# A four-layer trunk on one core: pooling bands made on GpSimd, a new order of the first loads and mixer steps, and last sums kept in PSUM

## Chip, core and metric

The kernel runs on one core of one Trainium2 chip. The metric is the device time of one execution in microseconds; less is better. Besides it the text uses one profiled execution, whose instructions are recorded with start, duration and what released them. Engines are named as in the profile: PE is TensorE, PEld its weight loads, DVE is VectorE, ACT is ScalarE, POOL is GpSimd, SP is SyncE, from which nearly all transfers are issued.

## The reference, cut to what matters

512 tokens of width 1024 go through two layers. The first mixes tokens by causal averages, the second by stick-breaking attention; a squared-ReLU MLP with 4096 hidden units follows each. All is float32, and RMS norms stand before and after each part:

```python
x = x + rms_norm(m, mix_post_g[layer])
h = rms_norm(x, mlp_pre_g[layer])
x = x + rms_norm(sq_relu_mlp(h, w_up[layer], w_down[layer]), mlp_post_g[layer])
```

The mixer of the first layer averages each of four groups of 256 channels over the last 2, 4, 8 or 16 tokens (fewer at the start of the sequence), subtracts the token itself, and applies a 256x256 linear map and a scale per channel:

```python
count = jnp.minimum(pos + 1, w).astype(jnp.float32)[None, :, None]
outs.append((upper - lower) / count - hf[:, :, sl])
...
y = jnp.einsum('bsgc,gcd->bsgd', y, w_grp.astype(jnp.float32)).reshape(B, S, D)
```

## The kernel before, in words

Tokens are cut into four tiles of 128 (`xt[0]` to `xt[3]`, kept on chip throughout). Float32 products of the MLPs and of the attention are made of three fast products of a high and a low part, so each operand is split by a ScalarE cast (high) and a VectorE subtraction (low).

**The mixer (lines 736 to 890).** An average over a window is a matrix product with a band: `own[t]` holds, for the four windows, 128 columns of weights for the tokens of the same tile and 16 columns for what reaches into the next tile (`BW` = 144, 576 columns in all). The bands come from the host as constants: one for tile 0, where the counts are smaller, and one for the later tiles, each 128 x 576 (lines 742, 750, 755). A tile's band is scaled by its inverse norm (line 809). `pooled` multiplies the tile with it (line 817), `copied` brings the result out of PSUM on ScalarE (line 827), `reached` adds the columns from the tile before (line 834), `mixed` applies the linear map (line 845), whose weights `pw` are first multiplied on VectorE by the gain and the scale (`linear`, line 788). The scale arrives as one row and is spread over the partitions by a product with ones (lines 777, 780). Norms run as ScalarE squares with an accumulator (line 301), two small GpSimd instructions (total, line 305, and power, line 312), and products on VectorE (349, 367, 403). Then tiles are transposed (411), split (421, 430) and meet the first up weights; `half_up` (line 870) starts four blocks of the first MLP on tiles 0 and 1.

The order of TensorE, ScalarE, VectorE and GpSimd in the mixer is written out in `MIX_ORDER` (line 45): each word is a step, a letter and indices. z: warm-up matmuls, so many; r, e: scale row and its copy; q, v, b: squares of x, inverse norm and scaled band of a tile; p, c, f, m: pooled, copied, reached and mixed of a tile and a part; w: linear weights of a half; s, g, V, a: squares, product with the gain, inverse norm and addition of the update; S, W, n: the same for the norm after it; t, h, l: transposes, high and low part; i, k: high and low part of an up weight, u: its product on half the tokens; X: like V, with its total on VectorE. Each engine takes its own steps in that order and waits at the head of its queue. Transfers are issued from SP in an order that the planner chose; the trace shows the two halves of x0, first band, scale row, x1, identity and gain columns (`eye`), first half of `pw`, second band, second half of `pw`, x2, x3, two gain rows, and then four up weights (lines 137 and 748 to 760, 857).

**The end (finish, line 466).** The second MLP's last partial sums are made in the order of `MLP_ORDER[1]` (line 99). p: products of a tile and a column group; v: their sum with the partial result `y` in SBUF, on VectorE, written to `y` (line 483); s: squares on ScalarE; g: product with the gain row on VectorE (line 349); V: inverse norm on GpSimd; a: addition to x on VectorE and the transfer of the result, issued from SP. Tile 3 has three column groups, of 512, 256 and 256, so that little is left after the last product; its sum of squares is made of the first two groups' total and the third's (line 361). VectorE's queue around the last tiles is v20, a10, a11, g20, v21, g21, v30, g30, v31, a20, v32, a21, g31, g32, a30, a31, a32.

Of the kernel before, what the change touches and what calls it, by code (L numbers as in the profile page):

```python
# [22 lines left out]
GRP = 4  # L23
# [6 lines left out]
WINDOWS = (2, 4, 8, 16)  # L30
EPS = 1e-6
TINY = 1e-24
TS = [slice(t * P, (t + 1) * P) for t in range(T)]
# [13 lines left out]
    for w in """z11 q00 r1 q01 v0 r0 q1 b0 v1 p00 b1 p01 p02 e0 e1 c01 c00 w0 w1 c02 p10 c10 q2 p12 q3 p11 m00 v2 s00 b2 c11 f10  # L47
    m01 v3 p21 p20 c12 s01 b3 c21 V0 p22 f11 c20 m10 g01 g00 m11 p32 c22 a00 i0 i2 a01 s10 f20 s11 k0 p31 S00 k2
    S01 p30 c30 g11 g10 V1 W0 a11 f21 a10 c32 n01 S11 m20 c31 n00 S10 f31 s20 m21 s21 W1 g20 g21 f30 V2 t01 n10
    t00 n11 h00 h01 m31 l01 a20 t10 s31 l00 h10 t11 m30 l10 h11 S20 i1 l11 g30 s30 a21 S21 V3 k1 W2 g31 a30 u0  # L50
    a31 i3 u1 n21 n20 S30 S31 W3 t21 n31 t20 u2 n30 t30 h20 k3 h21 t31 l21 h30 l20 l30 h31 l31 u3""".split()
# [38 lines left out]
def last_steps(text):  # L90
# [9 lines left out]
    p110123 v11 s11 g11 V1 p200123 v20 s20 a10 a11 g20 p210123 v21 s21 g21 V2 p300123 v30 s30 g30  # L100
    p310123 v31 s31 a20 p320123 v32 s32 V3 a21 g31 g32 a30 a31 a32"""),
# [9 lines left out]
def trunk(ctx, tc, x, consts, grow, pw, wup, wdn, wq, wk, wv, wo, out):  # L111
# [37 lines left out]
    def spare_tile():  # L149
        return work.tile([P, D], F32, tag="spare", name=name("spare"))  # L150

    def gain_row(r, t=None):
        t = work.tile([P, D], F32, tag="grow", name=name("grow")) if t is None else t
        nc.sync.dma_start(t, grow[r : r + 1, :].broadcast_to((P, D)))
        return t
# [172 lines left out]
    class Update:  # L328
        def __init__(self, t, gpost, scaled, eps=EPS, gpre=None, final=False, xn=None, gcol=None):

            self.t, self.gpost, self.scaled, self.eps = t, gpost, scaled, eps
            self.gpre, self.gcol, self.final = gpre, gcol, final
            self.xn = xn_tile() if xn is None else xn
            self.st = keep.tile([P, 8], F32, tag=f"stat{t}", bufs=4, name=name("stat"))
            self.summed = False
# [11 lines left out]
        def product(self, n, y):  # L347
            cut = self.cuts[n]
            return nc.vector.tensor_tensor(out=self.scaled[:, cut], in0=y, in1=self.gpost[:, cut], op=ALU.mult)
# [5 lines left out]
        def first_rstd(self):  # L355
            if len(self.cuts) == 2:
                if not self.summed:
                    self.first_total()
            else:
                both = self.st[:, 2:3]  # L360
                nc.gpsimd.tensor_tensor(out=both, in0=both, in1=self.st[:, 4:5], op=ALU.add)
            self.summed = False
            self.r = power(self.st, 0)

        def add_part(self, n):
            x, cut = xt[self.t], self.cuts[n]
            latest["dve"] = nc.vector.scalar_tensor_tensor(  # L367
                out=x[:, cut], in0=self.scaled[:, cut], scalar=self.r, in1=x[:, cut], op0=ALU.mult, op1=ALU.add
            )

# [95 lines left out]
    def finish(l, lhs, w, y, update):  # L466

        ups = [update(t, y[t]) for t in range(T)]
        bank = {}
# [11 lines left out]
        def evacuate(t, n):  # L481
            part = y[t][:, ups[t].cuts[n]]
            nc.vector.tensor_tensor(out=part, in0=bank.pop((t, n)), in1=part, op=ALU.add)  # L483

        def add(t, n):
            ups[t].add_part(n)
            if l == 1:
                cut = ups[t].cuts[n]
                nc.sync.dma_start(out[TS[t], cut], xt[t][:, cut])

        def transposes(t, h):
# [4 lines left out]
            "s": lambda t, n: ups[t].squares_of(n, y[t][:, ups[t].cuts[n]]),  # L496
            "g": lambda t, n: ups[t].product(n, y[t][:, ups[t].cuts[n]]),
# [238 lines left out]
    with tc.tile_pool(name="mix0", bufs=1, reuse_waits="tile") as mp:  # L736
        warm = mp.tile([P, 512], mybir.dt.bfloat16, tag="warm", name="warm")
        nc.gpsimd.memset(warm, 0.0)


        BW = P + max(WINDOWS)
        bands = [mp.tile([P, 4 * BW], F32, tag=f"band{i}", name=f"band{i}") for i in range(2)]

        row = mp.tile([P, D], F32, tag="row", name="row")
        nc.vector.memset(row, 0.0)
        ones = mp.tile([P, P], F32, tag="ones", name="ones")
        nc.gpsimd.memset(ones, 1.0)
        nc.sync.dma_start(row[:1], grow[R_SCALE : R_SCALE + 1, :])
        at = P + 4 * KC
        nc.sync.dma_start(bands[0], consts[:, at : at + 4 * BW])  # L750
        nc.sync.dma_start(xt[1], x[TS[1], :])
        nc.sync.dma_start(eye, consts[:, :at])
        wpool = [mp.tile([P, D], F32, tag=f"pw{i}", name=f"pw{i}") for i in range(2)]
        nc.sync.dma_start(wpool[0], pw[0])
        nc.sync.dma_start(bands[1], consts[:, at + 4 * BW :])
        nc.sync.dma_start(wpool[1], pw[1])
        nc.sync.dma_start(xt[2], x[TS[2], :])
        nc.sync.dma_start(xt[3], x[TS[3], :])
        gpost = gain_row(R_MIX_POST0)
        gpre0 = gain_row(R_MLP_PRE0, spare_tile())  # L760

# [44 lines left out]
        def band(t):  # L806

            own[t] = mp.tile([P, 4 * BW], F32, tag=f"own{t}", name=f"own{t}")
            nc.vector.tensor_scalar(
                out=own[t], in0=bands[min(t, 1)], scalar1=left.pop(("v", t)), scalar2=None, op0=ALU.mult  # L810
            )

        def pooled(t, i):
            left["p", t, i] = ps()
            for c, cb in enumerate(BLOCKS[i]):
                g = cb // 2
                nc.tensor.matmul(  # L817
                    left["p", t, i][:, c * BW : (c + 1) * BW], xt[t][:, cb * P : (cb + 1) * P],
                    own[t][:, g * BW : (g + 1) * BW], start=True, stop=True,
                )  # L820
# [47 lines left out]
        def half_up(j):  # L868
# [5 lines left out]
            "b": band, "p": pooled, "c": copied, "f": reached, "m": mixed,  # L874
# [10 lines left out]
        for j in range(GRP):  # L885
            load_up(j)
# [413 lines left out]
def constants(gains):  # L1300


    s, t = np.arange(P)[:, None], np.arange(P)[None, :]
    eye = (s == t).astype(np.float32)
    first, later = [], []
    for w in WINDOWS:
        inside = ((s <= t) & (s > t - w)).astype(np.float32)
        before = ((s - P > t - w).astype(np.float32) / np.float32(w))[:, : max(WINDOWS)]
        first.extend((inside / np.minimum(t + 1, w).astype(np.float32) - eye, before))
        later.extend((inside / np.float32(w) - eye, before))  # L1310
    return np.concatenate([eye, gains, *first, *later], axis=1).astype(np.float32)
# [43 lines left out]
```

## Time and profile before

| | us |
|---|---|
| median of three runs | 946.03 |
| lowest and highest | 945.78 and 946.63 |
| the profiled execution | 945.7 |
| its span, first to last instruction | 943.9 |

The page of the profile gives, for each engine, busy time, share of the span and number of instructions. Views of the trace list single instructions by time, group them by line, or tell what ended the idle time before them. In a row `L809` is a line of the kernel, `own<-band,stat` the tile written and the tiles read, `128x576 f32` partitions by elements. A matmul's recorded duration includes the time in which the next already runs.

### The profile page before, as it was taken

How to read it: one execution, taken by the hardware profiler on the slowest of the kernel's cores; microseconds unless marked ns; L12 is line 12 of the kernel's file. 1: busy time of each engine (PE TensorE's matmuls, PEld its weight loads, DVE VectorE, ACT ScalarE, POOL GpSimd, SP SyncE). 2: the span in 40 equal slices, each digit the busy share in tenths (PEclk: the TensorE clock that was granted, in tenths of full speed). 3: DMA queues.
4: the chain of work that ended last, by engine and by line, in shares of the span. 5: the costliest groups of instructions: out<-in, count | busy, mean ns of one | idle time of the engine just before them, and what ended most of it. 6: DMA issues, size and time to landing. Idle time of an engine off the chain costs nothing.

```text
span 943.9 us, 12327 instructions
## 1 busy us (share of the span) xinstructions
PE 934.5 (99%) x4691; PEld 788.0 (83%) x4691; DVE 696.4 (74%) x797; ACT 560.2 (59%) x983; POOL 40.5 (4%) x83
## 2 busy tenths in 40 slices
PE   9999999999999999999999999999999999999997
PEld 7998888888888888888889888898888888888886
DVE  5875799988979876268766388884696966958756
ACT  6568979788775547155545464875545444444532
POOL 2300000000000004000000001200000000000002
PEclk9999999999999999999999999999999999999999
DMA  8334969789697750633141271342414133133102
GB/s 311 138 138 154 342 218 356 287 280 356 216 329 283 281 195 2 223 134 134 72 178 64 107 273 45 141 150 97 172 45 148 76 133 112 45 134 112 39 7 90
DMA packets 43261, 156.14 MB, mean 165 GB/s; under 512 B 4289, under 2 KB 4673, under 8 KB 43202
## 3 DMA queue, kind: packets, MB, share of 16 engines
q1 hardware_dynamic: 43202, 155.36, 45.4%
q8 instruction: 37, 0.61, 0.3%
q14 instruction: 22, 0.18, 0.1%
HBM read 121.79 MB, written 33.55 MB: 165 GB/s over the span
## 4 chain that ended last, share of the span: by engine, by line
PE 97%; DMA 1%; DVE 0%; ACT 0%; POOL 0%; SPq 0%; issue 0%; POOLq 0%; DVEq 0%; ACTq 0%
PE ps L605 28%; PE ps L727 16%; PE ps L728 16%; PE ps L724 15%; PE ps L317 4%; PE ps L316 4%; PE ps L318 4%; PE ps L1064 2%; PE ps L1047 2%; PE ps L1089 2%; PE ps L845 1%; PE ps L411 1%; PE ps L817 1%; DMA band<-in_consts 1%; ACT xn L301 0%; DVE x L367 0%
## 5 line engine op out<-in xcount | busy, mean ns | idle before, releaser
L605 PE MATMUL ps<-w,a 128*128 128x512 f32 x1176 | 278.6, 389 | 0.0
L727 PE MATMUL ps<-xnh,w 128*128 128x512 f32 (+1 forms) x704 | 260.5, 372 | 0.0
L728 PE MATMUL ps<-xnl,w 128*128 128x512 f32 (+1 forms) x704 | 259.9, 370 | 0.0
L724 PE MATMUL ps<-xnh,w 128*128 128x512 f32 (+1 forms) x704 | 259.0, 370 | 0.0
L605 PEld LDWEIGHTS ps<-w,a 128*128 128x128 f32 x1176 | 220.7, 188 | 45.9 <-DVE w L298 0.2
L728 PEld LDWEIGHTS ps<-xnl,w 128*128 128x128 f32 x704 | 132.7, 188 | 22.3 <-DVE xnl L430 0.3
L724 PEld LDWEIGHTS ps<-xnh,w 128*128 128x128 f32 x704 | 132.1, 188 | 22.7
L727 PEld LDWEIGHTS ps<-xnh,w 128*128 128x128 f32 x704 | 132.2, 188 | 22.4
L614 DVE TENSOR_TENSOR y<-ps,y 128x512 f32<-128x512 f32 x124 | 84.3, 687 | 44.7 <-PE ps L605 44.4
L177 DVE TENSOR_TENSOR w<-raw,w 128x1024 fp32r<-128x1024 f32 x58 | 70.9, 1222 | 57.0 <-ACT w L175 56.8
L175 ACT CAST w<-raw 128x1024 fp32r<-128x1024 f32 x58 | 60.9, 1051 | 80.9 <-PE ps L724 79.5
L297 ACT CAST a<-r 128x768 fp32r<-128x768 f32 (+1 forms) x60 | 47.7, 794 | 71.8 <-PE ps L605 56.8
L298 DVE TENSOR_TENSOR a<-r,a 128x768 fp32r<-128x768 f32 (+1 forms) x60 | 54.0, 900 | 11.8 <-ACT a L297 11.6
L1028 DVE TENSOR_TENSOR_SCAN e<-u,begin 128x1280 f32<-128x1280 f32 x16 | 45.2, 2825 | 20.9 <-ACT u L1012 20.1
L297 ACT CAST w<-e 128x1536 fp32r<-128x1536 f32 (+1 forms) x30 | 41.8, 1395 | 22.7 <-DVE e L579 13.3
L298 DVE TENSOR_TENSOR w<-e,w 128x1536 fp32r<-128x1536 f32 (+1 forms) x30 | 49.4, 1647 | 1.8 <-ACT w L297 1.6
L187 ACT ACTIVATE apart<-apart,eye 128x128 f32<-128x128 f32 (+1 forms) x132 | 43.1, 408 | 0.0
L637 ACT ACTIVATE r<-ps 128x512 f32<-128x512 f32 x56 | 33.1, 591 | 8.7 <-PE ps L724 8.7
L298 DVE TENSOR_TENSOR w<-xn,w 128x1536 fp32r<-128x1536 f32 (+1 forms) x20 | 33.0, 1650 | 5.6 <-ACT w L297 5.5
L298 DVE TENSOR_TENSOR w<-w,w 128x1536 fp32r<-128x1536 f32 (+1 forms) x20 | 33.0, 1649 | 4.7 <-ACT w L297 4.7
L638 ACT ACTIVATE r<-r 128x512 f32<-128x512 f32 x56 | 35.5, 634 | 1.3
L301 ACT ACTIVATE xn<-y 128x512 f32<-128x512 f32 (+1 forms) x25 | 15.3, 614 | 31.6 <-DVE y L483 27.9
(134 smaller groups left out, 1321.4 us busy)
## 6 DMA issues: line engine op xcount, KB each, us to landing
raw<-in_wup SPq DMA_DIRECT2D x64, 512.0 KB, 4.1
w<-kept SPq DMA_DIRECT2D x60, 512.0 KB, 4.1
kept<-wx SPq DMA_DIRECT2D x30, 512.0 KB, 3.7
w<-in_wdn SPq DMA_DIRECT2D x8, 1536.0 KB, 6.6
kept<-apart SPq DMA_DIRECT2D x24, 512.0 KB, 5.7
xn<-in_wdn SPq DMA_DIRECT2D x8, 1536.0 KB, 7.4
apart<-in_wk SPq DMA_DIRECT2D x7, 512.0 KB, 7.2
apart<-in_wq SPq DMA_DIRECT2D x7, 512.0 KB, 9.5
```

The source lines that it names most:

```text
L175: nc.scalar.copy(hi, raw)
L177: nc.vector.tensor_tensor(out=lo, in0=raw, in1=hi.bitcast(F32), op=ALU.subtract)
L187: nc.scalar.mul(c, c, gc[:, at : at + 1])
L297: latest["act"] = nc.scalar.copy(hi, src)
L298: latest["dve"] = nc.vector.tensor_tensor(out=lo, in0=src, in1=hi.bitcast(F32), op=ALU.subtract)
L316: nc.tensor.matmul(dst, ah, bh, start=start, stop=False)
L605: nc.tensor.matmul(bank, a[:, x, q, TS[t]], w[:, z, q], start=start and q == 0 and k == 0, stop=q == self.n - 1 and k == 2, skip_group_che ...
L614: nc.vector.tensor_tensor(out=part, in0=bank, in1=part, op=ALU.add)
L724: nc.tensor.matmul(pu[:, cols], wl[:, k, :], xnh[:, k, cols], start=False, stop=k == KC - 1)
L727: nc.tensor.matmul(pu[:, cols], wh[:, k, :], xnh[:, k, cols], start=k == 0, stop=False)
L728: nc.tensor.matmul(pu[:, cols], wh[:, k, :], xnl[:, k, cols], start=False, stop=False)
L1028: nc.vector.tensor_tensor_scan(out=self.e[:, ::-1], data0=self.u[:, 1:][:, ::-1], data1=begin[:, ::-1], initial=0.0, op0=ALU.mult, op1=ALU ...
```

## The change

It has two parts that do not touch each other.

At the start, the bands are no longer sent from the host. VectorE fills `band` with the reciprocals of the windows, GpSimd cuts it to the band by one select over all four windows (below the diagonal) and one for each (beyond the window), makes a diagonal by another select, and VectorE subtracts it. What differs for the first 16 tokens is made in `first`, filled by 26 one-column memsets, and written over the first columns of tile 0's scaled band by a second instruction. The ones are filled by VectorE. The first loads are issued in a fixed order, and the four up weights only behind the last gain row. `MIX_ORDER` is listed anew, with eight warm-up matmuls in place of eleven and X0 in place of V0.

At the end, the sums of tiles 2 and 3 are written back into PSUM (`within`), where squares, gain product and addition read them. The sum of tile 3's two totals moves from GpSimd to VectorE. Tile 3's last column group is added to x by ScalarE (product with the inverse norm) and GpSimd (`add_apart`, step A); its second group's result is issued from ScalarE's queue. `MLP_ORDER[1]` places a20, a21 and g30 otherwise.

```diff
-    for w in """z11 q00 r1 q01 v0 r0 q1 b0 v1 p00 b1 p01 p02 e0 e1 c01 c00 w0 w1 c02 p10 c10 q2 p12 q3 p11 m00 v2 s00 b2 c11 f10
...
+    for w in """z8 q00 q01 v0 r0 q1 b0 r1 e0 v1 e1 p00 p01 b1 c00 c01 p02 q2 v2 p12 p11 w0 p10 c02 c11 w1 m00 m01 q3 c10 c12 b2
+    s01 s00 p21 v3 b3 g00 c21 p22 g01 f11 X0 p20 i0 m11 f10 a01 m10 a00 c20 p32 c22 i2 s11 g11 f20 k0 s10 S00
+    p31 S01 f21 V1 m21 p30 g10 W0 k2 a11 a10 m20 c31 c32 n01 S11 n00 f31 t00 c30 S10 s21 t01 s20 m31 g21 g20 h01
...
-    p110123 v11 s11 g11 V1 p200123 v20 s20 a10 a11 g20 p210123 v21 s21 g21 V2 p300123 v30 s30 g30
-    p310123 v31 s31 a20 p320123 v32 s32 V3 a21 g31 g32 a30 a31 a32"""),
+    p110123 v11 s11 g11 V1 p200123 v20 s20 a10 a11 g20 p210123 v21 s21 V2 g21 a20 p300123 v30 s30 a21 p310123
+    v31 s31 g30 p320123 v32 s32 g31 V3 g32 a30 A32 a31"""),
...
-                nc.gpsimd.tensor_tensor(out=both, in0=both, in1=self.st[:, 4:5], op=ALU.add)
+                nc.vector.tensor_tensor(out=both, in0=both, in1=self.st[:, 4:5], op=ALU.add)
...
+        def add_apart(self, n):
+            x, cut = xt[self.t], self.cuts[n]
+            part = self.scaled[:, cut]
+            nc.scalar.mul(part, self.held.pop(n), self.r)
+            nc.gpsimd.tensor_tensor(out=x[:, cut], in0=part, in1=x[:, cut], op=ALU.add)
...
+        def within(t):
+            return l == 1 and t >= T - 2
...
-            nc.vector.tensor_tensor(out=part, in0=bank.pop((t, n)), in1=part, op=ALU.add)
+            src = bank.pop((t, n))
+            total = sums[t, n] = src if within(t) else part
+            nc.vector.tensor_tensor(out=total, in0=src, in1=part, op=ALU.add)
...
+                issuer = nc.scalar if (t, n) == (T - 1, 1) else nc.sync
+                issuer.dma_start(out[TS[t], cut], xt[t][:, cut])
...
-        nc.sync.dma_start(bands[0], consts[:, at : at + 4 * BW])
-        nc.sync.dma_start(bands[1], consts[:, at + 4 * BW :])
+        with tc.manual_schedule(engines={mybir.EngineType.SP}):
+            nc.sync.dma_start(row[:1], grow[R_SCALE : R_SCALE + 1, :])
+            nc.sync.dma_start(xt[1], x[TS[1], :])
+            nc.sync.dma_start(wpool[0], pw[0])
+            nc.sync.dma_start(eye, consts)
+            nc.sync.dma_start(xt[2], x[TS[2], :])
+            nc.sync.dma_start(wpool[1], pw[1])
+            nc.sync.dma_start(xt[3], x[TS[3], :])
+            gpost = gain_row(R_MIX_POST0)
+            gpre0 = gain_row(R_MLP_PRE0, spare_tile())
...
+        band = mp.tile([P, NW, BW], F32, tag="band", name="band")
+        diagonal = mp.tile([P, P], F32, tag="diagonal", name="diagonal")
+        nc.gpsimd.memset(diagonal, 0.0)
+        nc.gpsimd.affine_select(
+            out=diagonal, in_=diagonal, pattern=[[-1, P]], base=0, channel_multiplier=1,
+            compare_op=ALU.not_equal, fill=1.0,
+        )
+        for g, w in enumerate(WINDOWS):
+            nc.vector.memset(band[:, g], 1.0 / w)
+        inside = band[:, :, :P]
+        nc.gpsimd.affine_select(
+            out=inside, in_=inside, pattern=[[0, NW], [1, P]], base=0, channel_multiplier=-1,
+            compare_op=ALU.is_ge, fill=0.0,
+        )
+        for g, w in enumerate(WINDOWS):
+            nc.gpsimd.affine_select(
+                out=band[:, g], in_=band[:, g], pattern=[[-1, BW]], base=w - 1, channel_multiplier=1,
+                compare_op=ALU.is_ge, fill=0.0,
+            )
+        first = mp.tile([P, NW, REACH], F32, tag="first", name="first")
+        nc.vector.memset(first, 1.0)
+        for g, w in enumerate(WINDOWS):
+            for c in range(w - 1):
+                nc.vector.memset(first[:, g, c : c + 1], float(np.float32(w) / np.float32(c + 1)))
+        nc.vector.tensor_tensor(out=first, in0=first, in1=band[:, :, :REACH], op=ALU.mult)
+        for part, n in ((first, REACH), (inside, P)):
+            same = diagonal[:, :n].unsqueeze(1).to_broadcast([P, NW, n])
+            nc.vector.tensor_tensor(out=part, in0=part, in1=same, op=ALU.subtract)
...
+            for dst, src in [(own[t], band)] + ([(own[t][:, :, :REACH], first)] if t == 0 else []):
+                nc.vector.tensor_scalar(out=dst, in0=src, scalar1=r, scalar2=None, op0=ALU.mult)
...
+        with tc.issue_after(rows[-1].ins):
+            for j in range(GRP):
+                load_up(j)
```

More of the change, by code (lines that the diff above doesn't have):

```diff
@@ L736, in trunk @@
     with tc.tile_pool(name="mix0", bufs=1, reuse_waits="tile") as mp:
+        row = mp.tile([P, D], F32, tag="row", name="row")
+        nc.vector.memset(row, 0.0)
         warm = mp.tile([P, 512], mybir.dt.bfloat16, tag="warm", name="warm")
         nc.gpsimd.memset(warm, 0.0)
[L741 to L745, printed above, removed]
@@ L756, in trunk @@
[L756 to L760, printed above, removed]
+        wpool = [mp.tile([P, D], F32, tag=f"pw{i}", name=f"pw{i}") for i in range(2)]
+        with tc.manual_schedule(engines={mybir.EngineType.SP}):
[8 more added lines that the diff above has]
+            gpre0 = gain_row(R_MLP_PRE0, spare_tile())
@@ L804, in first_norm, with own_band @@
             left["v", t] = power(stats[t], 0)
[L806 to L811, printed above, removed]
+        def own_band(t):
+            own[t] = mp.tile([P, NW, BW], F32, tag=f"own{t}", name=f"own{t}")
+            r = left.pop(("v", t))
+            for dst, src in [(own[t], band)] + ([(own[t][:, :, :REACH], first)] if t == 0 else []):
+                nc.vector.tensor_scalar(out=dst, in0=src, scalar1=r, scalar2=None, op0=ALU.mult)
         def pooled(t, i):
@@ L818, in pooled @@
                     left["p", t, i][:, c * BW : (c + 1) * BW], xt[t][:, cb * P : (cb + 1) * P],
[L819 removed]
+                    own[t][:, g], start=True, stop=True,
                 )
@@ L1300, in constants @@
 def constants(gains):
[L1303 to L1311, printed above, removed]
+    return np.concatenate([np.eye(P, dtype=np.float32), gains], axis=1).astype(np.float32)
 def kernel(x, pool_w, pool_scale, w_q, w_kv, kv_norm_g, w_o, w_up, w_down,
```

45 lines of the change are left out of this document (20 added, 25 removed).

## The prediction

> **What bounds the kernel now.** I read the page first (busy shares, clock, chain), then the waits of TensorE, then the timeline of the first 40 us and of the last 10, because the diff touches only these ends.
>
> ```profile
> span 943.9 us, 12327 instructions
> PE 934.5 (99%) x4691; PEld 788.0 (83%) x4691; DVE 696.4 (74%) x797; ACT 560.2 (59%) x983; POOL 40.5 (4%) x83
> PEclk9999999999999999999999999999999999999999
> PE 97%; DMA 1%; DVE 0%; ACT 0%; POOL 0%; SPq 0%; issue 0%; POOLq 0%; DVEq 0%; ACTq 0%
> ```
>
> Of TensorE's waits (total, times, longest us) one is more than 0.2 once the warm-up has begun:
>
> ```profile
> PE ps L817 <- DVE own L809: 0.9, 1, 0.9
> ```
>
> TensorE is 97% of the chain at full clock and waits once worth naming, at 10 us. The diff leaves its matmuls alone, but for three warm-up ones fewer. So the time is: when the real matmuls begin, plus their fixed length, plus holes, plus the tail after the last one. A microsecond gained in the first twelve arrives at the end unless a new hole takes it. The profiled execution took 945.7 us, 1.8 outside its span; the median is 946.03, so 0.3 is added to a sum made from this trace.
>
> **The start before.** In the timeline, columns are start, duration, engine, line, and the idle time before with its releaser:
>
> ```profile
> 1.03 0.91 DVE L745 MEMSET row<- 128x1024 f32 x1 [0.18 <-issue]
> 1.18 0.20 POOL L747 MEMSET ones<- 128x128 f32 x1
> 1.30 4.71 PE L772 MATMUL ps<-warm 128*128 128x512 bf16 x11 [1.30 <-POOL warm L738]
> 4.58 0.63 ACT L301 ACTIVATE junk<-x 128x512 f32<-128x512 f32 x1 [0.32 <-DMA x<-in_x]
> 5.40 0.29 POOL L305 TENSOR_SCALAR stat<-stat 128x1 f32<-128x1 f32 x1 [4.02 <-ACT junk L301]
> 5.78 0.57 POOL L312 TENSOR_TENSOR stat<-stat,mhalf 128x1 f32<-128x1 f32 x1
> 5.84 1.88 PE L777 MATMUL ps<-row,ones 128*128 128x512 f32 x4
> 6.38 0.52 DVE L809 TENSOR_SCALAR own<-band,stat 128x576 f32<-128x576 f32 x1 [4.43 <-POOL stat L312]
> 7.26 1.06 ACT L301 ACTIVATE junk<-x 128x1024 f32<-128x1024 f32 x1 [1.96 <-DMA x<-in_x]
> 7.56 2.12 PE L817 MATMUL ps<-own,x 128*128 128x144 f32 x16
> 10.04 0.52 DVE L809 TENSOR_SCALAR own<-band,stat 128x576 f32<-128x576 f32 x1 [3.14 <-DMA band<-in_consts]
> 10.48 3.25 DVE L788 SCALAR_TENSOR_TENSOR pw<-pw,eye,scale 128x256 f32<-128x256 f32 x8
> 10.62 2.23 PE L817 MATMUL ps<-own,x 128*128 128x144 f32 x16 [0.93 <-DVE own L809]
> 12.61 1.06 ACT L301 ACTIVATE junk<-x 128x1024 f32<-128x1024 f32 x1 [0.43 <-DMA x<-in_x]
> 20.22 1.05 ACT L862 CAST w<-raw 128x1024 fp32r<-128x1024 f32 x1 [0.58 <-DMA raw<-in_wup]
> ```
>
> Token tile 0's pooling (7.56) starts only behind the warm-up and the scale row (5.84 to 7.7), though its band was ready at 6.90. Tile 1's waits 0.93 for the second band table, landed at 10.0. After that there is no hole over 0.3 us.
>
> **Fewer bytes first.**
>
> ```profile
> x<-in_x SPq DMA_DIRECT2D x3, 512.0 KB, 7.6
> band<-in_consts SPq DMA_DIRECT2D x2, 288.0 KB, 5.1
> ```
>
> I take landings by bytes queued ahead. Five waits on DMA give a curve: 512 KB (x0) by 4.58, 1316 (x1) by 7.26, 2196 (second band) by 10.04, 3220 (x2) by 12.61, 6292 (third up weight) by 20.22 (gain rows, weights and pw halves are 512 KB like x, the identity 80, the scale row 4). Between them that is 300, 317, 398 and 404 KB per us. Without the bands and in the new order x1 closes 1028 KB, so 6.3; pw0 1540, 8.0; x2 2132, 9.8; pw1 2644, 11.2; x3 3156, 12.4; the first up weight 4692, 16.25. The scale row now stands ahead of everything but x0 on the fixed queue, and waits for its memset (ends 1.94); it stood ahead of x1 before as well. If the bands' bytes had cost nothing, x1 would stay at 7.26; the bytes decide, since the other waits on this list moved with them.
>
> **Bands made on the chip.** On GpSimd: one memset, a 128-column select, one of 512 columns, four of 144. The nearest rows stand in the attention set-up (duration min, median, max ns) and, in the groups of the first 46 us, in the mixer (busy us, mean ns of one):
>
> ```profile
> L985 POOL TENSOR_SCALAR_AFFINE_SELECT begin<-begin x4: 293/296/298, 375.1 to 375.9; 128x129 bf16<-128x129 bf16 x3, 128x128 bf16<-128x128 bf16 x1
> L981 POOL MEMSET begin<- x1: 1164/1164/1164, 373.7 to 373.7; 128x1280 bf16 x1
> ```
>
> ```profile
> L797 DVE MEMSET stat<- 128x1 f32 x3 | 0.1, 59 | 0.0
> L834 DVE TENSOR_TENSOR y<-y,y 128x64 f32<-128x64 f32 x6 | 1.3, 219 | 0.6 <-ACT y L827 0.6
> L349 DVE TENSOR_TENSOR m<-ps,grow 128x512 f32<-128x512 f32 x8 | 5.3, 685 | 0.2
> L845 PE MATMUL ps<-pw,y 128*128 128x256 f32 x64 | 14.6, 379 | 0.0
> L827 ACT COPY y<-ps 128x432 f32<-128x432 f32 x8 | 4.0, 520 | 1.5 <-PE ps L817 1.4
> ```
>
> From 128 to 1280 columns a GpSimd memset grows from 0.20 to 1.16, 0.84 ns a column. Low end: selects grow so from 0.296, hence 0.62 + 4 x 0.31 = 1.9. High end: all of a select is per column (2.3 ns), 1.2 + 4 x 0.33 = 2.5; if f32 counts double, 5. I take 2.3, since four bytes or two made no difference to the memset's rate. They can begin when VectorE has filled the band: 1.94 plus four memsets of about 0.17, so 2.65, and end at 4.95. VectorE's 26 single-column memsets (59 ns each, 1.6 us) end by 4.5, hidden by the selects. Then one product and one subtraction of 64 columns (0.22 each) and one subtraction of 512 (0.69): bands ready at 6.1. Tile 0's inverse norm was ready at 6.35; its total now meets that subtraction, which reads two SBUF operands, and such neighbours stretch GpSimd:
>
> ```profile
> 17.12 0.30 POOL L305 TENSOR_SCALAR stat<-stat 128x1 f32<-128x1 f32 x1 [0.89 <-ACT xn L301]
> 23.75 0.88 POOL L305 TENSOR_SCALAR stat<-stat 128x1 f32<-128x1 f32 x1 [0.28 <-ACT xn L301]
> ```
>
> The first ran beside VectorE's L349, which reads PSUM, the second beside L367, which reads SBUF alone. So 0 to 0.6 later; I take the scaled band to begin at 6.5, with 0.52 and another 0.22 for tile 0's first columns: 7.25, pooling from 7.3 instead of 7.56. The scale row, after eight warm-up matmuls (1.30 + 8 x 0.43 = 4.7), is done by 6.5 and hides in this. Gain 0.25.
>
> The Trainium skill (SBUF — State Buffer, "SBUF: two separate sides") says that VectorE and GpSimd share a port pair under an exclusive lock, taken by a VectorE instruction with two SBUF inputs, and that the loser blocks for the whole instruction. The pair of rows above agrees. By that rule the total would wait until 6.1 and the inverse norm until 6.75, and the sum would lose 0.25.
>
> **Tile 1 and the new list.** x1 at 6.3, squares with their accumulator about 1.2, total and power 0.95 (5.40 to 6.35), band 0.52: about 9.1. Tile 0's pooling takes 2.0 (its 2.12 less the last one's drain), until 9.3, so the hole of 0.93 closes. Then w0 runs on VectorE from 9.1 to 10.8 (four at about 0.41), under tile 1's pooling (to 11.3); w1 from 11.2 to 12.8 under the first mixing (8 matmuls, 14.6 us over 64, to 13.1). If w1 is late, m01 is, then p21 and all behind. b2 and b3 follow x2 and x3, whose squares end at 11.0 and 13.6. ScalarE's i0 now stands ahead of c20 and c22, so a late up weight would hold tile 2's copies, f20 and m20; five items of 0.5 to 0.6 (copies 0.52) lie between 13.6 and it, so it asks at 16.4, and its weight lands at 16.25. The margins are 0.2 to 0.3 us, so I subtract 0.1 for a hole. X0's sum on VectorE spares GpSimd 0.30 and hides under the pooling of tile 2. Later holes, three of 0.24 to 0.30 like this one, I leave:
>
> ```profile
> 32.54 0.19 PEld L728 LDWEIGHTS ps<-xnl,w 128*128 128x128 f32 x1 [0.26 <-DVE xnl L430]
> ```
>
> Start: 0.25 + 0.93 - 0.1 = 1.1 gained; bounds 0 and 1.5.
>
> **The tail.**
>
> ```profile
> 933.06 0.87 POOL L305 TENSOR_SCALAR stat<-stat,eps 128x1 f32<-128x1 f32 x1 [3.93 <-ACT xn L301]
> 936.78 0.28 PE L318 MATMUL ps<-dn,sq 128*128 128x256 f32 x1
> 937.10 0.42 DVE L483 TENSOR_TENSOR y<-ps,y 128x256 f32<-128x256 f32 x1 [0.35 <-PE ps L318]
> 937.56 0.42 ACT L301 ACTIVATE xn<-y 128x256 f32<-128x256 f32 x1 [0.87 <-DVE y L483]
> 937.88 0.19 ACT L301 ACTIVATION_READ_ACCUMULATOR xn<-y 128x1 f32 x1
> 938.22 0.35 POOL L361 TENSOR_TENSOR stat<-stat 128x1 f32<-128x1 f32 x1 [1.05 <-ACT xn L301]
> 938.64 0.63 POOL L312 TENSOR_TENSOR stat<-stat,mhalf 128x1 f32<-128x1 f32 x1
> 939.31 1.54 DVE L367 SCALAR_TENSOR_TENSOR x<-xn,stat,x 128x512 f32<-128x512 f32 x3 [0.45 <-POOL stat L312]
> ```
>
> Up to the accumulator (938.07) nothing changes, if a PSUM result costs VectorE what an SBUF one does; no row shows one, bounds 0 and 0.1 each. VectorE must be free at 937.10. Its queue now holds a20 before v30 and g30 before v32; a20 waits for V2, and v30, s30 and g30 stand behind it. V2's total (933.06) took 0.87 beside a product from SBUF; the product now reads PSUM, so 0.4, and with 0.1 and 0.56 for the power a20 can go at 934.1. The last two groups are 12 matmuls at 0.12, so v31 is ready 1.44 before 937.10 and v30 2.88 before, at 934.2. a20 ends at 934.8, v30 at 935.5, a21 at 936.1, v31 at 936.5, g30 at 937.1. It just fits; with V2 as slow as before, v32 is 0.5 late. The sum of the two squares moves from GpSimd (0.35 and the hop) to VectorE (a 128x1 memset is 0.06): power from 938.2 to 938.8, not 939.27. Gain 0.45. After it VectorE adds 512 and 256 columns (0.74, 0.40) instead of 512, 256 and 256, done at 939.95; ScalarE scales the last 256 (0.4) and GpSimd adds them from 939.3. That add is not shown: low end 0.35 (L361, one column), high end 0.35 + 512 reads at 2.3 ns, 1.5. I take 0.7, between the ends, as the select rate is nearer in kind. It ends at 940.0, before at 940.85. Outputs go on two queues. Gain 0.85, bounds 0 and 0.95.
>
> The Trainium skill (GPSIMD Engine Reference, "Elementwise — side-by-side cycle accounting") warns that GpSimd's two-input add is about half as fast as VectorE's, 4497 ns at 2048 columns. An estimate from that is 0.56 for 256, and the gain would be 0.9; no run here shows it.
>
> Sum: 1.1 + 0.85 = 1.95. 945.7 - 1.95 = 943.75; with 0.3, **944.05**.
>
> **Rivals.** (1) The bands come late: the selects wait for VectorE's memsets until 4.5 and end at 6.8, bands at 7.9, pooling at 8.8, tile 1's at 10.8 where it was 10.62. The start loses 0.2: 945.4. For it speak the rows 17.12 and 23.75; against it, L747: GpSimd's memset took 0.20 beside VectorE's. (2) The other side: the f32 select with its patterns costs 4 times the rate of L985: 9.2 ns a column, 1088 columns, 10.0 us. Bands at 13.8, pooling at 14.6, tile 1's at 16.6, the start loses 6.0: 951.2. Slower by over 1.9 begins where the start loses 2.75, that is with bands at 10.5 or 6 ns a column. For it, only a two-byte, one-row pattern is on record; against it, that row's 0.296 repeats within 5 ns. (3) The new list makes holes: i0 or w1 waits on DMA, 1 us; 945.05. The row at 20.22 shows the kind; the byte curve speaks against it. (4) GpSimd's add at its high end ends at 940.8: 944.85. (5) The list also closes the holes at 32 to 40 us, 0.8: 943.25. (6) V2 stays slow and v32 is 0.5 late: 944.55.
>
> **Chances.** The forecast 0.52, own range 943.4 to 944.9; rivals (1) 0.11, (2) 0.12, (3) 0.08, (4) and (6) together 0.05, (5) 0.12. No change to be told is within 0.2%, 1.9 us, so faster begins below 944.14: some three fifths of the forecast and all of (5), 0.44. Slower is (2) and a remnant, 0.14. The rest, 0.42, is same. The range, 943.1 to 946.2, leaves out (2) and little beside.
>
> **What would show it.** Right: no idle before the second pooling group, pooling from about 7.3; selects of 0.3 and about 0.8; x1's squares from 6.3; the last add on GpSimd about 2.9 us after the last matmul. Wrong: TensorE waiting for own at tile 0 beyond 8; a hole in L845 behind pw or raw; L483 late by L367 at the last column group.

## The result, and the profile after

The changed kernel takes 947.33 us (median of 20 runs, 947.0 to 947.94), the kernel before 945.8 in the same session (945.4 to 947.63): ratio 1.0015, interval 1.0008 to 1.0022. It is slower by 1.5 us, where 944.05 was forecast and 943.1 to 946.2 given as the range. The profiled execution took 947.35 us, with a span of 945.6 (before: 945.7 and 943.9). Of the runs further below, three single executions far from the rest (2847 us in new_list, 1168 in lows_late and in one_queue) are left out of the medians.

TensorE's waits in the changed kernel (in total, times, longest, us):

```profile
PE ps L820 <- POOL warm L761: 1.4, 1, 1.4
PE ps L425 <- DVE xn L417: 1.3, 2, 0.8
PE ps L894 <- DVE stat L307: 0.9, 1, 0.9
PE ps L866 <- DVE stat L845: 0.7, 1, 0.7
```

The first belongs to the warm-up and was there before. The last is tile 1's pooling, the wait of 0.93 that the change was to close. The two between them are new, 2.2 us together, and neither waits for a transfer. The timeline of the changed kernel (start, duration, idle time before it and what ended that) shows where they lie:

```profile
2.71 0.64 POOL L789 TENSOR_SCALAR_AFFINE_SELECT band<-band 128x512 f32<-128x512 f32 x1 [0.89 <-DVE band L785]
3.42 1.10 POOL L794 TENSOR_SCALAR_AFFINE_SELECT band<-band 128x144 f32<-128x144 f32 x4
4.96 0.69 DVE L808 TENSOR_TENSOR band<-band,diagonal 128x512 f32<-128x512 f32 x1
5.00 0.81 POOL L307 TENSOR_SCALAR stat<-stat 128x1 f32<-128x1 f32 x1 [0.48 <-ACT junk L303]
6.50 0.52 DVE L860 TENSOR_SCALAR own<-band,stat 128x576 f32<-128x576 f32 x1 [0.86 <-POOL stat L314]
7.37 2.23 PE L866 MATMUL ps<-own,x 128*128 128x144 f32 x16
7.52 1.06 ACT L303 ACTIVATE junk<-x 128x1024 f32<-128x1024 f32 x1 [2.62 <-DMA x<-in_x]
10.33 2.23 PE L866 MATMUL ps<-own,x 128*128 128x144 f32 x16 [0.74 <-DVE stat L845]
17.35 1.29 DVE L355 TENSOR_TENSOR m<-ps,grow 128x512 f32<-128x512 f32 x2 [1.65 <-ACT xn L303]
18.92 3.69 PE L894 MATMUL ps<-pw,y 128*128 128x256 f32 x16 [0.94 <-DVE stat L307]
28.72 1.09 PE L425 MATMUL ps<-eye,xn 128*128 128x128 f32 x8 [0.47 <-DVE xn L417]
40.70 1.23 PE L425 MATMUL ps<-eye,xn 128*128 128x128 f32 x8 [0.82 <-DVE xn L417]
```

The bands are on time: the selects end at 4.52, the subtraction at 5.65, the scaled band begins at 6.50 and the pooling at 7.37. But ScalarE gets x1 only at 7.52, not at 6.3, so tile 1's pooling is 0.29 earlier than before (10.62) instead of 0.93. Then TensorE stands at 18.92, 28.72 and 40.70, before a mixing product and before the transposes of tiles 0 and 2. The row at 17.35 names the other side of the first one: VectorE idled 1.65 us for a square of ScalarE before it could make the product g00.

The end of the changed kernel:

```profile
938.66 0.28 PE L320 MATMUL ps<-dn,sq 128*128 128x256 f32 x1
938.97 0.43 DVE L503 TENSOR_TENSOR ps<-ps,y 128x256 f32<-128x256 f32 x1
940.02 0.16 DVE L367 TENSOR_TENSOR stat<-stat 128x1 f32<-128x1 f32 x1 [0.28 <-ACT xn L303]
940.26 0.56 POOL L314 TENSOR_TENSOR stat<-stat,mhalf 128x1 f32<-128x1 f32 x1 [0.90 <-DVE stat L367]
940.86 1.14 DVE L374 SCALAR_TENSOR_TENSOR x<-ps,stat,x 128x512 f32<-128x512 f32 x2 [0.34 <-POOL stat L314]
941.40 0.73 POOL L383 TENSOR_TENSOR x<-xn,x 128x256 f32<-128x256 f32 x1 [0.58 <-ACT xn L382]
942.03 0.41 ACTq L510 DMA_DIRECT2D out<-x  x1
```

The last matmul ends at 938.94 (938.66 + 0.28), before at 937.06: 1.88 later. From there to the end of the span it is 6.66 us, before 6.84. So of the 1.7 us by which the span grew, the last matmul brings 1.9 and the new end takes 0.2 off. From the start of tile 1's pooling to the end of the last matmul it is 928.60 us, before 926.45: behind that pooling 2.15 us were added, about the sum of the new waits.

### The profile page after: what moved, and what is told of

Read it like the earlier page. It is cut to its first block, busy times and chain, and to the rows that moved or that the text cites. A ratio compares the mean times of both kernels' runs of the same rounds, so it can differ in the third digit from the quotient of the medians.

```text
span 945.6 us, 12363 instructions
## 1 busy us (share of the span) xinstructions
PE 934.3 (99%) x4688; PEld 788.1 (83%) x4688; DVE 698.5 (74%) x834; ACT 559.7 (59%) x984; POOL 44.2 (5%) x88
## 4 chain that ended last, share of the span: by engine, by line
PE 93%; DVE 1%; POOL 1%; ACT 1%; issue 0%; POOLq 0%; ACTq 0%
PE ps L626 28%; PE ps L748 15%; PE ps L749 15%; PE ps L745 15%; PE ps L318 4%; PE ps L320 4%; PE ps L319 4%; PE ps L1114 2%; PE ps L1097 2%; PE ps L1139 2%; PE ps L425 1%; ACT xn L303 1%; DVE x L374 0%; POOL stat L307 0%; POOL stat L314 0%
## 5 line engine op out<-in xcount | busy, mean ns | idle before, releaser
L307 POOL TENSOR_SCALAR stat<-stat,eps 128x1 f32<-128x1 f32 x8 | 5.5, 682 | 632.6 <-ACT xn L303 632.6
```

## The experiments

Each run is compared with the kernel before, run on the same chip beside it (945.6 to 945.7). All carry the new end; they differ from the changed kernel, or from one another, as the diffs say.

| run | median, us | ratio to before, interval | last matmul ends | to it from tile 1's pooling |
|---|---|---|---|---|
| end_only | 945.31 | 0.9998 (0.999 to 1.0007) | 936.95 | 926.27 |
| old_list | 945.43 | 0.9995 (0.9986 to 1.0004) | 937.32 | 926.28 |
| new_list | 948.19 | 1.0029 (1.0018 to 1.0039) | 939.39 | 928.69 |
| fold_first | 947.53 | 1.0019 (1.001 to 1.0028) | 939.26 | 928.33 |
| lows_early | 945.99 | 1.0003 (0.9994 to 1.0013) | 938.11 | 926.94 |
| lows_late | 947.65 | 1.0019 (1.001 to 1.0028) | 938.07 | 928.26 |
| x1_ahead | 945.55 | 1.0 (0.9991 to 1.0009) | 936.01 | 926.35 |
| no_first_store | 945.22 | 0.9996 (0.9987 to 1.0005) | 937.38 | 926.22 |
| g30_early | 945.23 | 0.9994 (0.9985 to 1.0003) | 937.67 | 926.49 |
| one_queue | 945.62 | 1.0001 (0.9992 to 1.001) | 937.24 | 926.52 |
| no_row | 945.31 | 0.9994 (0.9985 to 1.0003) | 936.82 | 926.21 |
| x1_halves | 944.79 | 0.9989 (0.998 to 0.9998) | 936.01 | 926.19 |

The last two columns are of one profiled execution, which is not the median's, and x1 lands at another time in each. The last one, from the start of tile 1's pooling to the end of the last matmul, takes x1's landing out: in the eight profiles with the order of before, that of the kernel before among them, it lies between 926.19 and 926.52.

**The square (old or new loads, old or new order): which part costs the time.** In end_only the start, loads, bands and list are those of before. old_list is the changed kernel with the order of before (and eight warm-up matmuls); new_list is end_only with the new order.

```diff
-    for w in """z8 q00 q01 v0 r0 q1 b0 r1 e0 v1 e1 p00 p01 b1 c00 c01 p02 q2 v2 p12 p11 w0 p10 c02 c11 w1 m00 m01 q3 c10 c12 b2
+    for w in """z8 q00 r1 q01 v0 r0 q1 b0 v1 p00 b1 p01 p02 e0 e1 c01 c00 w0 w1 c02 p10 c10 q2 p12 q3 p11 m00 v2 s00 b2 c11 f10
...
```

> The kernel before with the change's end alone (sums held in PSUM, last update on three engines, the second queue); start, loads, bands and mixer list are as before. Theory A, from the two traces: the last store is issued 0.6 us earlier behind the last matmul, but its landing takes 0.5 us longer, so the time comes out 0.0 to 0.2 us under 945.8, and TensorE's last matmul still ends at 937.1. Theory B, the prediction's tail: 0.85 us less, 944.95; the slow landing in the changed kernel was then an accident of that kernel's timing and is not seen here.

> The changed kernel with the mixer steps in the order of before (8 warming matmuls kept, since 11 would run past the bands). Theory L, the list makes the holes: the waits of 1.11 us before 18.9, 0.64 before 28.7 and 0.97 behind 39.6 go back to the 0.2 to 0.3 us ones of before, the start keeps its 0.3 us, the last matmul ends near 936.8 and the time is 945.4 (945.0 to 945.7). Theory D, the loads make them (x1 and the constants land later than before, the DMA engines stand partly idle at 2 to 5 us): holes of the same sum stay wherever the list is, and the time is 946.8 to 947.4.

> The kernel before, its loads and its loaded bands, with the new list of mixer steps and the new end: the other corner of the square. Theory L: the holes behind s00/g00/f11 and behind tile 2's and tile 3's norms are there on the old loads as well, some 2.1 us, the last matmul ends at 938.8 to 939.3 (the start's 0.3 us is lost) and the time is 947.3 to 947.9. Theory D: the old loads feed the new list, the holes are no larger than before and the time is 945.3 to 946.

By median, with the old list the new loads and bands change nothing (945.31 and 945.43), while the new list costs 2.9 us on the old loads (948.19) and 1.9 on the new ones (947.33). From tile 1's pooling on, the two prices are nearly one: 2.4 us (928.69 less 926.27) and 2.3 (928.60 less 926.28). Theory L holds. end_only itself is nearer theory A than B: 0.3 us of its span is gained behind the last matmul. TensorE's waits in new_list are those of the changed kernel, on loads and bands of before:

```profile
PE ps L425 <- DVE xn L417: 1.3, 2, 0.8
PE ps L838 <- DVE stat L818: 1.3, 1, 1.3
PE ps L866 <- DVE stat L307: 0.9, 1, 0.9
```

and the first and last of these are gone in old_list, whose only large wait is tile 1's pooling (1.4 of the 1.8; the rest is tile 0's). First its row among the waits, then the one in the timeline:

```profile
PE ps L866 <- DVE own L860: 1.8, 2, 1.4
11.03 2.23 PE L866 MATMUL ps<-own,x 128*128 128x144 f32 x16 [1.44 <-DVE own L860]
```

old_list is the 945.4 expected, but no better than end_only: the 0.3 us that theory L allowed the new start is not there. In its profile x1 landed at 8.14, later than in any of the five profiles with the loads of before (7.17 to 7.79).

**A hole closed, and another in its place.** fold_first changes one stretch of the new list:

```diff
-    s01 s00 p21 v3 b3 g00 c21 p22 g01 f11 X0 p20 i0 m11 f10 a01 m10 a00 c20 p32 c22 i2
+    s00 s01 p21 v3 b3 f11 g00 c21 p22 g01 X0 p20 m11 f10 a01 m10 a00 c20 p32 c22 i0 i2
```

> The changed kernel with one stretch of its list altered: the fold f11 ahead of the products g00 and g01, the squares s00 ahead of s01, and the copy i0 of the first up weight moved behind the copies c20 and c22. Theory L in its small form, that VectorE standing behind s00 is what held m11: the wait of 1.11 us before 18.9 falls under 0.3, and if nothing further on is late anyway the last matmul ends 0.8 to 1.0 earlier, at 937.9, time 946.4. The rival: the later holes (tile 0's and tile 2's norms) wait on the same chain of VectorE and GpSimd work, so that what is won at 18.9 is lost again before 40, and the time stays within 0.2 of 947.3.

The hole before 18.9 went, and the time did not move (947.53): the rival. VectorE's wait went to the next product, and TensorE's with it:

```profile
22.14 0.69 DVE L355 TENSOR_TENSOR m<-ps,grow 128x512 f32<-128x512 f32 x1 [1.88 <-ACT xn L303]
24.38 1.97 PE L894 MATMUL ps<-pw,y 128*128 128x256 f32 x8 [1.13 <-DVE y L883]
```

Why that is so stands in the busy times by stretches of 4 us. First the changed kernel, then old_list (in each: the stretch, then its length, and the busy time of PE, PEld, DVE, ACT and POOL, with the number of instructions in brackets):

```profile
15.00:19.00 4.00, 3.06 (x22) 2.77 (x21) 2.17 (x6) 2.95 (x8) 0.17 (x2) 1.00 1.03 420
19.00:23.00 4.00, 4.00 (x21) 3.59 (x22) 2.81 (x6) 2.43 (x6) 0.52 (x1) 1.00 0.20 73
23.00:27.00 4.00, 4.00 (x24) 3.55 (x24) 3.79 (x6) 3.04 (x11) 3.22 (x4) 1.00 0.38 131
27.00:31.00 4.00, 3.52 (x21) 2.89 (x20) 3.75 (x7) 3.28 (x10) 2.88 (x5) 1.00 0.00 0
31.00:35.00 4.00, 4.00 (x28) 3.69 (x27) 4.00 (x8) 3.02 (x6) 0.07 (x1) 1.00 0.01 2
```

```profile
15.00:19.00 4.00, 4.00 (x27) 3.74 (x27) 2.84 (x7) 3.38 (x9) 2.34 (x5) 1.00 1.03 421
19.00:23.00 4.00, 4.00 (x24) 3.64 (x23) 3.79 (x6) 3.52 (x8) 0.05 (x1) 1.00 0.39 125
23.00:27.00 4.00, 4.00 (x24) 3.64 (x24) 3.55 (x7) 3.95 (x12) 2.83 (x5) 1.00 0.29 104
27.00:31.00 4.00, 4.00 (x28) 3.43 (x27) 3.94 (x9) 2.84 (x9) 2.01 (x4) 1.00 0.00 0
31.00:35.00 4.00, 4.00 (x28) 3.56 (x27) 4.00 (x8) 3.29 (x8) 0.08 (x1) 1.00 0.01 2
```

From 23 to 35 us VectorE is nearly full in both (3.5 to 4.0 of 4). In the eight microseconds ahead of that it works 4.98 us in the changed kernel (2.17 + 2.81) and 6.63 in old_list, although old_list's tile 1 began 0.7 later: 1.65 us are lost there that nothing later can take up. In the old order VectorE makes k0 and k2, the low parts of two up weights (line 915, 1.22 us each), while ScalarE's squares are out; in the new one they stand behind g11, which waits for s11.

**The test of that.** lows_early takes fold_first and puts f20, f21, k0 and k2 ahead of g11 (its diff follows); lows_late does the opposite to old_list: f20, k0 and k2 go behind g11. A fold is a step f, the addition of `reached`.

```diff
-    a01 m10 a00 c20 p32 c22 i0 i2 s11 g11 f20 k0 s10 S00
-    p31 S01 f21 V1 m21 p30 g10 W0 k2 a11
+    a01 m10 a00 c20 p32 c22 i0 i2 f20 f21 k0 k2 s11 g11 s10 S00
+    p31 S01 V1 m21 p30 g10 W0 a11
```

> The changed kernel with the list of the run before it (fold f11 first, i0 later) and VectorE's folds f20, f21 and remainders k0, k2 ahead of the product g11, so that VectorE has work while ScalarE's square s11 is still out. Theory V: TensorE's holes are VectorE time lost at 15 to 23 us (it idled 1.65 to 1.88 us there for squares and was full from 23 to 35); filled with the 2.4 us of k0 and k2, the holes at 23 and the one of 1.0 at 40 both go, the last matmul ends near 937.3 and the time is 945.2 to 945.8. Rival G: the hole at 40 is tile 2's own chain through GpSimd's power and stays; only the one at 23 goes, 946.2 to 946.6. Rival M: a hole moves once more, 947.3.

> The mirror of it: the changed kernel with the order of before (run old_list, 945.4), in which only f20, k0 and k2 are put behind the product g11, as the new list has them. Theory V: VectorE idles for s11 instead of doing 2.4 us of remainders, is full later, and TensorE gets holes of 1.0 to 2.0 us before 45 us; time 946.4 to 947.4. Rivals: were it another part of the new list (the order of the squares, the later a20 and a21), the time would stay at 945.4.

lows_early took 945.99, 1.5 us less than fold_first, between the ranges of theory V and rival G: the hole before 24.4 is gone. The one before tile 2's transposes stayed, so rival G was right about that one:

```profile
PE ps L866 <- DVE stat L845: 1.6, 1, 1.6
PE ps L425 <- DVE xn L417: 0.9, 1, 0.9
```

lows_late took 947.65, a little more than expected (from tile 1's pooling 928.26, old_list 926.28), and the old order got the new one's hole: VectorE stands 2.68 us for the square, the folds stand behind it and TensorE behind them.

```profile
21.72 0.69 DVE L355 TENSOR_TENSOR m<-ps,grow 128x512 f32<-128x512 f32 x1 [2.68 <-ACT xn L303]
26.36 1.97 PE L894 MATMUL ps<-pw,y 128*128 128x256 f32 x8 [1.70 <-DVE y L883]
```

**The last hole.** g30_early moves one more step of lows_early: g30 from behind a31 to ahead of it.

```diff
-    k1 S20 W2 a31 g30 a30
+    k1 g30 S20 W2 a31 a30
```

> Run lows_early with one step moved: VectorE's product g30 ahead of the update a31 instead of behind it, so that it runs in the 0.85 us in which VectorE waits for GpSimd's power. Theory V: tile 2's norm then starts 0.68 us sooner (at 38.3 in that run's time), and TensorE's wait of 1.02 us before tile 2's transposes falls to 0.3 to 0.4, as in the order of before; median 0.4 to 0.7 under lows_early's, 945.3 to 945.6. Rival G, tile 2's chain waits for GpSimd's second power (it ended at 38.05): the wait stays over 0.8 and the time is 946.0.

It took 945.23, and TensorE's wait for xn of line 417 is no longer among its waits. Tile 2's norm had not waited for GpSimd, as rival G had it, but for g30 (0.68) in front of it, which fits into the 0.85 us that VectorE spent waiting for the power. The intervals of lows_early and g30_early overlap; the traces tell them apart. From tile 1's pooling on, the new order's price goes step by step: 928.60 (changed kernel), 928.33 (fold_first), 926.94 (lows_early), 926.49 (g30_early). The last lies among the values of the old order, so that the new order costs nothing any more that these runs can tell.

**When x1 lands.** x1_ahead is old_list with tile 1 asked for first on SP, and the scale row on ScalarE's queue. no_row takes the row's load away from that and fills the row with a constant, so that the pooling scale is one. x1_halves loads and squares tile 1 in two halves.

```diff
+        nc.scalar.dma_start(row[:1], grow[R_SCALE : R_SCALE + 1, :])
         with tc.manual_schedule(engines={mybir.EngineType.SP}):
-            nc.sync.dma_start(row[:1], grow[R_SCALE : R_SCALE + 1, :])
             nc.sync.dma_start(xt[1], x[TS[1], :])
```

```diff
-            nc.sync.dma_start(xt[1], x[TS[1], :])
+            for cut in NS:
+                nc.sync.dma_start(xt[1][:, cut], x[TS[1], cut])
...
-    v0 r0 q1 b0 v1
+    v0 r0 q10 b0 q11 v1
```

> Run old_list (new loads, new bands, order of before, 945.4) with tile 1 asked for first on SP, at 1.63 us instead of 2.40, and the scale row asked for on ScalarE's queue behind its memset. Theory I, the issue sets x1's landing: x1 lands 0.7 us earlier than the 7.44 to 8.14 of the runs so far, 6.9 to 7.3, tile 1's pooling begins near 10.2 and the time falls to 944.7 to 945.0. Rival S: x1 and the pooling weights share the 16 DMA engines and x1 lands with the bytes of both, at 7.4 or later whatever the issue; the time stays within 0.2 of 945.4.

> Run x1_ahead without the load of the scale row: the row is filled with a constant on the chip, so that the pooling scale is taken as one. In every trace so far one to three of a transfer's 16 shares fall 0.5 to 2 us behind the others in the transfer that follows the row, and every later transfer carries that. Theory R, the one-partition row holds up the DMA engines it lands on: without it the last share of each load comes within 0.4 us of the median, the pooling weights land at 7.4 instead of 8.43, and the times keep within 0.5 us of each other near 944.4. Rival N, the lag is not the row's (4 KB packets, or other traffic): the spread of the shares and of the times (944.4 to 947.2) stays.

> Run x1_ahead with tile 1 loaded and squared in two halves of 512 columns, as tile 0 is. Its last half's square takes 0.6 us instead of 1.06, so where x1 is late tile 1's pooling begins some 0.45 us sooner; the other loads are asked for 0.4 us later. If a late x1 is what spreads x1_ahead's times (median 945.55, fastest 944.44): median 944.9 to 945.3. If the spread comes from the loads behind it: 945.5 to 945.9.

A load comes in 16 shares, each of which completes by itself; the consumer waits for the last (in the changed kernel x1's last share is there at 7.44, its square begins at 7.52). From the completions in the traces (us; x1's issue, then first, median and last share):

```
              issue  first  median  last
before         2.47   5.94    6.56  7.17
changed        2.40   5.63    6.16  7.44
old_list       2.40   5.81    6.18  8.14
lows_early     2.39   6.05    6.27  8.27
x1_ahead       1.70   5.28    5.53  6.05
no_row         1.70   5.25    5.49  7.71
```

Two things are apart here. The median share goes with the issue: 0.7 earlier for x1_ahead and no_row. The rates of the DMA engines in slices of 0.3 us (GB/s, from 0 to 12 us) show the same, first for the changed kernel, then for x1_ahead:

```profile
GB/s 0 0 0 0 0 0 102 273 376 403 362 225 130 177 246 191 191 273 423 396 410 352 318 299 349 350 370 379 411 369 369 396 410 369 423 437 410 369 328 369
```

```profile
GB/s 0 0 0 0 0 0 143 218 294 376 341 280 294 321 355 355 355 300 287 273 330 349 314 424 384 364 372 399 369 423 410 437 423 410 437 423 396 410 369 314
```

In the changed kernel the rate falls to 130 at 3.6 us. SP asks for the row when VectorE's memset of it ends (2.01), at 2.04, and for x1 behind it, at 2.40. The five other profiles with that order of issue have the same dip, to 55 to 137; the three with x1 at 1.70 do not go under 225 there. In the kernel before x1 was asked for no sooner (2.47), but the first band's bytes came between, and the rate there was 227 or more.

The last share is another matter: one to six of the 16 come more than 0.5 and up to 2.2 us behind the median, in one execution more than in the next, and the following loads of that execution mostly carry the delay on. It is not the row's doing: no_row has it as well (7.71), and its times spread from 944.03 to 947.21. So x1_ahead lands x1 at 6.05 in its profile and has no hole left at tile 1, but its median is no better than old_list's, its runs reaching from 944.44 to 947.17. The profiled execution is the fastest of them; that late shares make the others slower is likely, but not shown. Theory I was right about the issue, wrong about the median.

x1_halves took 944.79, a little better than expected, with runs from 944.45 to 945.51. Its second half landed at 7.36 in the profile, as late as x1 in the changed kernel, and still tile 1's pooling begins at 9.82, where the changed kernel began at 10.33, and waits a quarter of a microsecond:

```profile
9.82 2.23 PE L867 MATMUL ps<-own,x 128*128 128x144 f32 x16 [0.23 <-DVE own L861]
```

It is the only version whose interval lies on the fast side of the kernel before, if barely (0.9998): new bands, new end, old order, tile 1 first and in halves. That the halves bring it, and not the early issue alone, the times do not show: x1_ahead's interval overlaps.

**The end.** no_first_store is end_only without the store of the last tile's first half, which is left out of the output; one_queue is end_only with all stores on SP.

```diff
-                issuer.dma_start(out[TS[t], cut], xt[t][:, cut])
+                if (t, n) != (T - 1, 0):
+                    issuer.dma_start(out[TS[t], cut], xt[t][:, cut])
```

```diff
-                issuer = nc.scalar if (t, n) == (T - 1, 1) else nc.sync
-                issuer.dma_start(out[TS[t], cut], xt[t][:, cut])
+                nc.sync.dma_start(out[TS[t], cut], xt[t][:, cut])
```

> The kernel before with the new end (run end_only, 945.3), without the store of the last tile's first half (256 KB): that part of the output is not written. It asks whether the last store's slow landing (2.3 to 2.4 us after its issue, 1.86 before the change) is the 512 KB that the new end asks for within 0.9 us. Theory B, bytes: the last landing comes 1.9 us after its issue or sooner and the time is 0.3 to 0.5 under end_only, 944.8 to 945.0. Rival Q: the second queue or the late GpSimd write has a fixed price; landing still 2.3 us after issue, time 945.3.

> Run end_only (945.3) with all stores on SP's queue again; sums in PSUM and the last update on three engines stay. Theory Q, two stores asked for within 0.13 us on two queues delay each other: the last store is issued 0.3 us later, lands 1.9 to 2.0 us after it instead of 2.26, and the time is the same within 0.1. Theory W, the second queue is worth its 0.3 us: 945.6, last landing still 2.2 or more after its issue.

no_first_store took 945.22, the same as end_only within the intervals. In its trace the last store still lands 2.07 us after its issue, between end_only's 2.26 and the 1.86 of before: theory B's saving does not show in the time, but the bytes may have a part in the slow landing. In one_queue the last store is issued 3.6 us behind the last matmul instead of 3.2, and lands sooner after its issue (1.87). The transfers of the last microseconds (count, size, median us from issue to landing), first of end_only, then of one_queue:

```profile
out<-x SPq DMA_DIRECT2D x1, 128.0 KB, 2.3
```

```profile
out<-x SPq DMA_DIRECT2D x2, 128.0 KB, 1.9
```

So theory Q: 6.55 us from last matmul to end with two queues, 6.66 with one. The medians, 945.31 and 945.62, differ by more than that, but their intervals overlap. The Trainium skill (DMA: Bandwidth & Descriptors, "Issuing engines are not separate DMA queues") says that all issuing engines use the same 16 DMA engines and that a second one saves only the sequencer's issue time. The pair agrees as to the issue, of which 0.38 us were saved. That 0.39 us came back in the landing is the pair's own finding.

## Why the prediction was wrong

By the profiles the change was to gain 1.95 us and lost 1.65. Of these 3.6 us the list has 2.15 (behind tile 1's pooling), the start 0.8 (up to it) and the tail 0.7 (behind the last matmul).

*What bounds the kernel.* Right, and it is why a list of steps can cost 2 us: TensorE is dense, and a hole in the first 45 us arrives at the end.

*The new list* is the step that failed. The prediction checked the margins of w0, w1 and i0 against transfers, subtracted 0.1 for a hole, and left the later ones as they were. The list itself put three holes there, 2.2 us by the waits, and the square of runs puts its price at 1.9 (new loads) to 2.9 (old loads) by the medians, at 2.3 to 2.4 from tile 1's pooling. Rival (3) had the kind, a list that makes holes, but with the wrong waiter (i0 or w1 on DMA) and 1 us. What was not read from the profile of before is that VectorE has next to no slack from 23 to 35 us. The busy times of the kernel before (columns as above) had it:

```profile
23.00:27.00 4.00, 4.00 (x23) 3.54 (x22) 3.54 (x7) 3.78 (x12) 2.92 (x4) 1.00 0.25 102
27.00:31.00 4.00, 4.00 (x27) 3.49 (x26) 3.94 (x9) 3.00 (x8) 1.58 (x4) 1.00 0.00 0
31.00:35.00 4.00, 4.00 (x28) 3.60 (x27) 4.00 (x7) 3.30 (x8) 0.50 (x1) 1.00 0.01 4
```

It works 11.5 of those 12 us, so that each wait at the head of its queue in the stretch before counts in full. fold_first shows that closing TensorE's hole alone does not help; lows_early and lows_late show that VectorE's wait is what counts, by filling it and by putting it into the old order.

*Fewer bytes first.* Wrong in the size. x1 landed at 7.44 instead of 6.3; 576 KB fewer brought the first up weight 0.3 us earlier (17.35), not 1.4. Landings do not follow the bytes queued ahead alone: the fixed order asks for x1 hardly sooner (2.40, before 2.47), behind a row that waits for its memset, and the last share decides. The curve was drawn through landings of one execution, in which the late shares were already contained.

*Bands made on the chip.* Right: selects with gaps 1.81 us where 2.3 were taken, the scaled band from 6.50 as forecast, pooling from 7.37 (7.3). Rivals (1) and (2) did not come. The total of tile 0's norm took 0.81, beside a subtraction of VectorE that reads SBUF twice, and ended 0.16 after it. By the lock that the Trainium skill (SBUF — State Buffer, "SBUF: two separate sides") states, GpSimd waits for that subtraction; the rows agree, and as the subtraction ended at 5.65 instead of 6.1, the wait cost nothing against the forecast.

*Tile 1.* The hole was to close; it shrank from 0.93 to 0.74, and in other executions with the same loads it was anything from under 0.1 (lows_late, x1 at 6.91) to 1.6 (g30_early, x1 at 8.29). Start: 0.3 gained instead of 1.1, before the list's holes.

*The tail.* Right in kind, too large in size: 0.85 forecast, 0.18 measured (0.13 to 0.29 over the profiles with both queues, by span less last matmul, without the one that leaves out a store). The engines' part brought 0.6: the last add ends 3.19 us after the last matmul, 3.79 before. GpSimd's add took 0.73 (0.7 forecast; the Trainium skill's GPSIMD Engine Reference, "Elementwise — side-by-side cycle accounting", gave the estimate 0.56). The power came 0.1 later after the last matmul than forecast, and ScalarE's product and the add took 0.1 more. Of the 0.6, 0.4 was lost in the landing, for which the sum had no term: the last store lands 2.38 us after its issue, before 1.86. Two stores are asked for within 0.13 us on two queues; with one queue it is 1.87. VectorE was free at the last column group, as forecast: its sum starts 0.03 after the last matmul, and writing the sum to PSUM in place of SBUF cost it nothing (0.43 against 0.42). Rivals (4) and (6) did not come.

## What to carry to other kernels

Before an order of steps is listed anew, look at each engine's busy time in stretches: where a side engine is nearly full for 12 us, a wait at the head of its queue shortly before that is as dear as a wait of the bounding engine, and closing TensorE's hole only moves it. Give such an engine something independent to do while it waits (here two low parts of 1.22 us, or one 0.68 us product). What the first work waits for is worth asking for first, and perhaps in pieces, so that only the last piece stands behind a late share; the second half of this is suggested by x1_halves, not shown apart.

## What was not expected of the hardware

A load's 16 shares do not end together: the last ran up to 2.2 us behind the median (7.71 against 5.49 in no_row), in six kernels with the same first loads by 0.95 to 2.2, and the following loads kept most of the distance. What makes the share late stays open; no_row shows that it needs no transfer of the row. Whether rows of 2 KB instead of 4 KB helped x1_halves, beside the shorter last square, was not tried apart.

26 memsets of one column, costed at 59 ns each (1.6 us), ran into one another and took 0.38 in all:

```profile
2.92 0.38 DVE L804 MEMSET first<- 128x1 f32 x26
```
